# Experts in a fixed order with 8 KB weight pieces and pads, and eight modulation blocks moved from beside attention

## The chip, the cores and the metric

The kernel runs on one core of one Trainium2 chip. The metric is the time of one execution on the device in microseconds (us). Times of several runs are given by their median, with the lowest and the highest. Profiles are of one execution each. The engines are PE (TensorE; PEld is its weight load), DVE (VectorE), ACT (ScalarE), POOL (GpSimd) and SP (SyncE, which here only issues transfers).

## The reference

Two blocks of a network in float32 on 512 tokens of width 1024. The first: modulated norm, differential attention of 4 heads over 768 keys, a Fourier mix, and 32 experts with two chosen per token. The second: an S5 mixer with a gated linear unit (glu), an MLP, an SSD mixer and a second MLP, each behind a modulated norm. Cut to what the change touches:

```python
def expert_block(args):
    tok, wt, e = args
    xb = h_pad[tok]
    y = (jax.nn.silu(xb @ w_gate[e]) * (xb @ w_up[e])) @ w_down[e]
    return y * wt[:, None]
...
out = jnp.zeros((t + 1, d), ys.dtype).at[buf_tok].add(ys.reshape(-1, d))
...
mod = cond @ ada_w[i] + ada_b[i]
sh1, sc1, g1, sh2, sc2, g2 = jnp.split(mod[:, None, :], N_MOD, axis=-1)
h = _modulate(_rmsnorm(x, norm_mix_g[i]), sh1, sc1)
...
ab = g @ w_glu.astype(f32) + b_glu.astype(f32)
val, gate = jnp.split(ab, 2, axis=-1)
return (val * jax.nn.sigmoid(gate)).astype(h.dtype)
```

`w_gate` and `w_up` are 32 x 1024 x 512, `w_down` is 32 x 512 x 1024, `ada_w` is 2 x 1024 x 6144.

## The kernel before, in words

The program runs its stages one after the other: `pre` (modulation, the input projection, attention, Fourier mix, output projection, router), `moe` (the experts), `end_first` (the first block's result is transposed and normed), `s5` with the glu, an MLP, the SSD mixer, an MLP, and the last norm.

**The experts** (`moe`, L916). They are taken in 16 pairs; two pairs make a step `st` of four experts. Each expert has 64 places for tokens, so a pair fills 128: expert A the columns 0 to 63 of PE's array, B the columns 64 to 127, with a matmul of its own for each (L970, L1001: "tiled"). A pair's work on PE, with the names that the profile shows: `G` and `U` (the products with gate and up, 32 records each: an fp32 matmul is two), `phT` (L982, four transposes of the gated product), `pw` (L988, each place's gate weight), `Y` (L1001, the products with down in two halves of 512 columns), `pohT` (L1012, four transposes of the one-hot matrix), and the combine `pcmb` (L1019, L1020): eight output blocks of two matmuls, each added by DVE to the residual `x` (L1022). ACT copies between them: `sg` (L978), `hT` (L984), `yh` (L1006), `ohT` (L1014). The second pair of a step also gathers the tokens of the next step, `pg` (L910, L911): four quarters of 16 matmuls, which ACT copies to `xg` with scale and shift (L914).

**What lies beside the experts.** A generator `self.blocks` (`s5_blocks`, L1496) makes tables for the S5 stage, one block per pair. It has three small groups on PE, `pcd`, `pm` and `pkt` (L1518, L1543, L1550), table work on DVE (`m`, `pb`, `tmpm`), copies `Cd`, `me` and `kt` on ACT, and stores by POOL's queue.

**What sets the order.** The code states data dependencies and the framework's scheduler places each engine's instructions, so groups of one pair and of the next are mixed. `issue_after` holds an item back behind a named instruction. PSUM has eight banks: in this stage one pool of 7 for all products and one bank, `psz`, for `pcd`, `pm`, `pkt` and the modulation.

**Weights.** `raw` (L125) takes a slot of a ring of six (8 KB per partition each) and issues the load on SP (L127). A 1 MB load of an expert's half matrix takes rows as `(k p)`: 512 runs of 2 KB, four to each partition. The first two loads of `w_down` go to two buffers `extra` (L937).

**Modulation** (`ada_quads`, L350). The first block's modulation and that of the second block's first layer are products of a vector with a 1024 x 6144 matrix, in blocks of 512 columns: four loads of 512 KB (tile `adaw`, 1 KB runs) and for each four matmuls `ada` (L364; 8 records). The generator `self.side` yields once per block; `values`, `keys`, `queries` and `attention` take one at each `next`, so that these loads and matmuls lie beside attention. Their buffers, `adap`, are two. `glu` (L1739) follows products of `gemm_T` (L162) on `w_s_glu`, 48 matmuls each.

## Time and profile before

| | us |
|---|---|
| median of 3 runs (lowest to highest) | 2454.11 (2452.0 to 2458.82) |
| the profiled execution | 2456.05 |
| its span | 2454.3 |
| PE busy | 2281.1 (93%) |
| DVE busy | 1353.9 (55%) |
| ACT busy | 816.7 (33%) |
| POOL busy | 240.2 (10%) |
| moved by DMA | 454.02 MB, 185 GB/s over the span |

Times in the trace count from the start of the span. A record's busy time includes what overlaps its neighbours (matmuls are pipelined), so the pace of matmuls is read from start to start. The chain that ended last lies for 54% of the span on PE. The page's shares are means over stages with different limits, so each stage is read by itself. "Idle before, and the releaser" in a row says what an engine was waiting for: a wait for several things is put down to the one that came last. SP's waits are for free buffers.

### The profile page before, as it was taken

Reading aid. Unit: us, or ns where it says so; the run is one execution under the profiler, and the core shown is the slowest. Engines: PE = TensorE matmul, PEld = TensorE weight load, DVE = VectorE, ACT = ScalarE, POOL = GpSimd, SP = SyncE. Lnnn points to the kernel's source line nnn. Section 1 sums busy time; section 2 is a strip of 40 time slices with the busy share of each in tenths; the row PEclk is TensorE's granted clock in tenths of the full one; section 3 lists DMA queues with packets and bytes.
Section 4 is the critical chain, followed back from the end, with each engine's and each line's share of the span. In section 5 each row is a group of like instructions: output and inputs, shape, how many; then the busy total and the mean of one; then the engine's idle time right before and its main releaser. Section 6 shows DMA issues by size and latency. Waiting matters only on the chain.

```text
span 2454.3 us, 32253 instructions
## 1 busy us (share of the span) xinstructions
PE 2281.1 (93%) x12503; PEld 1633.9 (67%) x12503; DVE 1353.9 (55%) x2583; ACT 816.7 (33%) x1317; POOL 240.2 (10%) x407
## 2 busy tenths in 40 slices
PE   7988999699998999979999999999999998999997
PEld 4664569344444444368788778787778777888787
DVE  4754445424334242466667884466786778544454
ACT  4232343211111111154333332335654434322332
POOL 0166000011111010000000000000221210000000
PEclk9899999899999999989999999999999999999999
DMA  8577645699999999945545772342332322233330
GB/s 282 163 219 235 196 141 189 248 326 341 355 377 322 331 331 355 340 132 160 175 125 169 228 229 91 95 123 62 112 104 87 111 78 86 69 95 95 94 96 35
DMA packets 327775, 454.02 MB, mean 185 GB/s; under 512 B 22308, under 2 KB 201252, under 8 KB 327620
## 3 DMA queue, kind: packets, MB, share of 16 engines
q1 hardware_dynamic: 318272, 435.23, 53.8%
q0 software_dynamic: 8592, 16.27, 2.1%
q8 instruction: 100, 1.64, 0.3%
q10 hardware_dynamic: 756, 0.43, 0.1%
q14 instruction: 55, 0.45, 0.1%
HBM read 436.14 MB, written 15.73 MB: 184 GB/s over the span
## 4 chain that ended last, share of the span: by engine, by line
PE 54%; DVE 8%; DMA 3%; ACT 3%; issue 2%; POOL 0%; SPq 0%; DVEq 0%; ACTq 0%; POOLq 0%
PE pt L146 13%; PE pt L147 13%; PE pt L148 13%; PE G L970 3%; PE Y L1001 3%; PE U L970 3%; DMA adaw<-in_ada_w 3%; DVE adaacc L314 1%; DVE wl L140 1%; PE pg L910 1%; PE pg L911 1%; PE py L1925 1%; PE pY L1668 0%; DVE x L1327 0%; PE pG L1637 0%
## 5 line engine op out<-in xcount | busy, mean ns | idle before, releaser
L140 DVE TENSOR_TENSOR wl<-w,wh 128x1024 fp32r<-128x1024 f32 (+2 forms) x239 | 287.4, 1207 | 225.1 <-ACT wh L139 221.0
L139 ACT ACTIVATE wh<-w 128x1024 fp32r<-128x1024 f32 (+1 forms) x241 | 249.0, 1040 | 480.5 <-PE pt L147 375.1
L146 PE MATMUL pt<-hh,wh 128*128 128x512 f32 (+2 forms) x976 | 369.0, 383 | 3.2 <-ACT hh L1219 3.0
L147 PE MATMUL pt<-hl,wh 128*128 128x512 f32 (+2 forms) x976 | 367.9, 380 | 0.1
L148 PE MATMUL pt<-hh,wl 128*128 128x512 f32 (+2 forms) x976 | 365.9, 378 | 0.0
L146 PE MATMUL pt<-ab,wh 128*128 128x512 f32 (+1 forms) x576 | 213.4, 375 | 4.8 <-ACT o L1347 2.9
L147 PE MATMUL pt<-ab,wh 128*128 128x512 f32 (+1 forms) x576 | 214.4, 373 | 1.1 <-DVE ab L1296 0.9
L148 PE MATMUL pt<-ab,wl 128*128 128x512 f32 (+1 forms) x576 | 213.7, 372 | 0.0
L146 PEld LDWEIGHTS pt<-hh,wh 128*128 128x128 f32 (+1 forms) x976 | 181.9, 188 | 44.9 <-ACT hh L1219 4.2
L147 PEld LDWEIGHTS pt<-hl,wh 128*128 128x128 f32 (+1 forms) x976 | 182.9, 188 | 39.3 <-issue 3.6
L148 PEld LDWEIGHTS pt<-hh,wl 128*128 128x128 f32 (+1 forms) x976 | 183.0, 188 | 39.0 <-issue 3.5
L1327 DVE SCALAR_TENSOR_TENSOR x<-pt,mod,x 128x512 f32<-128x512 f32 (+1 forms) x184 | 122.3, 678 | 115.2 <-PE pt L148 114.5
L970 PE MATMUL G<-w,xg 128*64 128x512 f32 x512 | 131.8, 602 | 5.3 <-DVE x L1022 5.3
L979 DVE TENSOR_TENSOR sg<-sg,U 128x512 f32<-128x512 f32 x16 | 11.0, 688 | 227.6 <-PE U L970 227.6
L970 PE MATMUL U<-w,xg 128*64 128x512 f32 x512 | 131.1, 594 | 0.0
L146 PEld LDWEIGHTS pt<-ab,wh 128*128 128x128 f32 x576 | 108.2, 190 | 30.2 <-ACT ab L1295 7.6
L147 PEld LDWEIGHTS pt<-ab,wh 128*128 128x128 f32 x576 | 109.4, 190 | 23.3 <-DVE ab L1296 3.5
L148 PEld LDWEIGHTS pt<-ab,wl 128*128 128x128 f32 x576 | 109.3, 190 | 19.9
L1914 POOL TENSOR_TENSOR ec<-ec,BC 128x384 f32<-128x384 f32 x32 | 39.9, 1263 | 686.7 <-PE pt L148 571.3
L970 PEld LDWEIGHTS G<-w,xg 128*64 128x64 f32 x512 | 38.0, 137 | 75.9 <-issue 63.0
L970 PEld LDWEIGHTS U<-w,xg 128*64 128x64 f32 x512 | 40.8, 137 | 70.7 <-issue 69.2
L1022 DVE TENSOR_TENSOR x<-x,pcmb 128x512 f32<-128x512 f32 x128 | 80.5, 673 | 4.7 <-PE pcmb L1020 4.7
(575 smaller groups left out, 4236.5 us busy)
## 6 DMA issues: line engine op xcount, KB each, us to landing
w<-in_w_gate SPq DMA_DIRECT2D x64, 1024.0 KB
w<-in_mlp_w SPq DMA_DIRECT2D x128, 512.0 KB
w<-in_w_up SPq DMA_DIRECT2D x63, 1024.0 KB
extra<-in_w_down SPq DMA_DIRECT2D x32, 1024.0 KB
w<-in_w_down SPq DMA_DIRECT2D x31, 1024.0 KB
adaw<-in_ada_w SPq DMA_DIRECT2D x48, 512.0 KB
adaw<-in_ada_w SPq DMA_DIRECT2D x96, 256.0 KB
w<-in_m_w_in SPq DMA_DIRECT2D x40, 512.0 KB
```

The lines of the kernel that those rows point to most:

```text
L139: nc.scalar.activation(h, w, AF.Copy)
L140: (eng or nc.vector).tensor_tensor(l, w, h.bitcast(F32), op=SUB)
L146: nc.tensor.matmul(out, ah, bh, start=start, stop=False, skip_group_check=True)
L147: nc.tensor.matmul(out, ah, bl, start=False, stop=False, skip_group_check=True)
L148: return nc.tensor.matmul(out, al, bh, start=False, stop=stop, skip_group_check=True)
L314: nc.vector.scalar_tensor_tensor(acc, w, ck, acc, op0=MUL, op1=ADD)
L910: nc.tensor.matmul(pt[:, i], self.h2h[:, t, ks], oh2d[:, t], start=(t == 0), stop=False)
L970: nc.tensor.matmul(pt[64 * i:64 * i + 64], xg[:, kh * 4 + k, so + 64 * i:so + 64 * i + 64], ws[i][:, k], start=(kh == 0 and k == 0), stop= ...
L1001: ip = nc.tensor.matmul(pt[64 * i:64 * i + 64], hT[:, k, 64 * i:64 * i + 64], ws[i][:, k], start=(k == 0), stop=(k == 3), tile_position=(0 ...
L1022: nc.vector.tensor_tensor(xs, xs, pt, op=ADD)
L1327: self.nc.vector.scalar_tensor_tensor(xs, src, gate, xs, op0=MUL, op1=ADD)
L1914: nc.gpsimd.tensor_tensor(ec, ec, BC[:, 1, 128:512], op=MUL)
```

## The change

Four parts.

1. **8 KB pieces.** Row `d` of a matrix is now `p*8+k` (`p*4+k` for down), so that a partition's part of a half matrix is one run of 8 KB, 128 runs for a megabyte. A half of `w_down` is now half of its rows at full width, so both Y banks fill together and end together. The order of rows inside the operands follows: `h2h`, `h2l` are written from strided reads, the scale and shift columns are turned through a transpose and a DRAM tile, `hm` reads `sg` and `U` with stride 4.
2. **Fixed order.** Each PE instruction of the experts and the S5 blocks gets, by `pin`, a dependency without a semaphore on the one before it in the program. The combine of a pair moves into the next pair: two output blocks after each of the four half products of G and U. `pw` moves behind the first half of G, in fp32r with the weights split in two (four matmuls in one pass in place of four in two). Two gather quarters lie in each pair, one before and one after `phT` (none in the first pair, four in the second, none in the last two). `pohT` is a product with an fp32r identity. S5 blocks are yielded in thirds. PSUM: tag `a` 2 banks, `gu` 3 (G, U, Y), `c` 2 (combine), `psz` 1.
3. **Modulation.** Of the 12 blocks of the second block's first layer eight leave attention: four loads behind the transposes in `end_first`, four before the first S5 scan, and eight after each of three glu products. They take slots of the weights' ring (`rawp`). What stays is taken four loads at a time, at half of attention's places.
4. **Pads.** Small tiles `shift`, `shift2`, `shift3` move the addresses of what follows them.

```diff
+    def pin(self, i):
+
+        if self.pinned:
+            if self.line is not True:
+                self.tc.add_manual_dep(i.ins, self.line.ins.name, mybir.DependencyInfo(
+                    mybir.DependencyClass.NoSync, mybir.DependencyReason.DATA), reason="pin")
+            self.line = i
+        return i
...
-    def ada_quads(self, items):
+    def ada_quads(self, items, tile, total):
...
-                        w = self.adap.tile([128, 4, 256], F32, tag="w", name="adaw")
+                        w = tile()
...
+                        if (b, k0, hf) != (nb - 1, 4, 1):
+                            yield
...
+    def sides(self, n):
+        for _ in range(n):
+            next(self.side, None)
...
-        ada = [(a["w_ada"][0], 0, n, mcol[:, n * 4 - 16:n * 4], self.col["bada"][:, n * 4:n * 4 + 16]) for n in (4, 8)]
-        ada += [(a["ada_w_2"][0], 1, n, mod0[:, n * 4:n * 4 + 16], self.col["bada0"][:, n * 4:n * 4 + 16]) for n in (0, 4, 8)]
+        ada = [(a["w_ada"][0], 0, n, 4, mcol[:, n * 4 - 16:n * 4], self.col["bada"][:, n * 4:n * 4 + 16]) for n in (4, 8)]
+        ada0 = [(a["ada_w_2"][0], 1, n, m, mod0[:, n * 4:(n + m) * 4], self.col["bada0"][:, n * 4:(n + m) * 4])
+                for n, m in ((0, 4), (4, 2), (6, 4), (10, 2))]
...
-        next(self.blocks)
+        for _ in range(4):
+            next(self.blocks)
...
+        pt = self.psum_z((16, 128), name="psp")
+        nc.tensor.transpose(pt, mcol[:, 8:24], self.ident)
+        rows = tp.tile([16, 128], F32, tag="ssr", name="ssr", bufs=1)
+        nc.scalar.activation(rows, pt, AF.Copy)
+        ssd = self.dr.tile([16, 128], F32, name="ssd")
+        nc.sync.dma_start(ssd, rows)
+        ssp = self.g.tile([128, 2, 8], F32, name="ssp")
+        nc.sync.dma_start(ssp, ssd.rearrange("(c r) (q k) -> (r q) c k", c=2, k=8))
+        self.sh2, self.sc2 = ssp[:, 0], ssp[:, 1]
...
+        xk = lambda t, k: x1[:, t].rearrange("s (p k) -> s k p", k=8)[:, k]
+        by_k = lambda h, t, k: h[:, t].rearrange("s (k p) -> s k p", k=8)[:, k]
...
+        self.mods2_scale(0, mod0, 8, "nmix")
+
+        self.side = self.ada_quads(ada0[1:], lambda: self.rawp.tile([128, 4, 256], F32, tag="raw", name="adaw"),
+                                   lambda: self.nrm.tile([128, 512], F32, tag="sq", name="adaacc"))
...
-                next(self.side, None)
+                self.sides(4)
...
-            next(self.side, None)
+            if t % 2 == 0:
+                self.sides(4)
...
         def part(wt, e, kh, q=None):
-            return self.raw(wt[e, kh * 512:(kh + 1) * 512].rearrange("(k p) n -> p k n", p=128), (128, 4, 512), q=q)
+            return self.raw(wt[e].rearrange("(p k) n -> p k n", k=8)[:, 4 * kh:4 * kh + 4], (128, 4, 512), q=q)
...
-        down = lambda e, hf: wd[e, :, hf * 512:(hf + 1) * 512].rearrange("(k p) n -> p k n", p=128)
+        down = lambda e, kh: wd[e].rearrange("(p k) n -> p k n", k=4)[:, 2 * kh:2 * kh + 2]
         xg2 = self.B((128, 2, 2048), name="xg")
-        place = lambda w: w.rearrange("p (k n) -> p k n", k=4)
+        place = lambda w: w.rearrange("p (k n) -> p k n", k=2)
...
-                return self.raw(down(e, hf), (128, 4, 512))
+                return self.raw(down(e, hf), (128, 2, 1024))
...
+            gu = lambda n: self.ps.tile([128, 512], F32, tag="gu", name=n, bufs=3)
+            pin = self.pin
+            self.line = self.pinned = True
...
+            def combine(ohT, yh, yl):
+
+                for t in range(4):
+                    for hf in range(2):
+                        pt = self.ps.tile([128, 512], F32, tag="c", name="pcmb")
+                        ls = ohT[:, t * 128:(t + 1) * 128]
+                        pin(nc.tensor.matmul(pt, ls, yh[:, hf], start=True, stop=False))
+                        pin(nc.tensor.matmul(pt, ls, yl[:, hf], start=False, stop=True))
+                        xs = x1[:, t, hf * 512:(hf + 1) * 512]
+                        nc.vector.tensor_tensor(xs, xs, pt, op=ADD)
+                        yield
...
+            ident_r = mp.tile([128, 128], F32R, name="ident_r", bufs=1)
+            nc.scalar.activation(ident_r, self.ident, AF.Copy)
+
+            gw2 = mp.tile([128, 4, 8, 2, 4], F32R, name="gw2", bufs=1)
+            gw4 = self.gw.rearrange("p t (s e) -> p t s e", e=4)
+            nc.scalar.activation(gw2[:, :, :, 0], gw4, AF.Copy)
+            nc.vector.tensor_tensor(gw2[:, :, :, 1], gw4, gw2[:, :, :, 0].bitcast(F32), op=SUB)
...
+                    quarters = [(nxt[1], nxt[0], 256, (k, k + 2)) for k in range(0, 8, 2)] if st < 7 else []
+                    quarters = quarters[2 * pr:2 * pr + 2] if st else quarters[:4 * pr]
+                    G, U = gu("G"), gu("U")
...
-                                    nc.tensor.matmul(pt[64 * i:64 * i + 64], xg[:, kh * 4 + k, so + 64 * i:so + 64 * i + 64],
-                                                     ws[i][:, k], start=(kh == 0 and k == 0), stop=(kh == 1 and k == 3),
-                                                     tile_position=(0, 64 * i), skip_group_check=True)
-                    for i in range(4):
-                        if pr == 1 and st < 7:
-                            self.gather(nxt[1], nxt[0], 256, (2 * i, 2 * i + 2))
-                    sg = mp.tile([128, 512], F32, tag="sg", name="sg")
-                    hm = sg
+                                    pin(nc.tensor.matmul(pt[64 * i:64 * i + 64],
+                                                         xg[:, kh * 4 + k, so + 64 * i:so + 64 * i + 64], ws[i][:, k],
+                                                         start=(kh == 0 and k == 0), stop=(kh == 1 and k == 3),
+                                                         tile_position=(0, 64 * i), skip_group_check=True))
+                            for _ in range(2):
+                                next(back, None)
+                            if (w is wg) and kh == 0:
+
+                                pw = self.psum((128, 2, 4), name="pw")
+                                for t in range(4):
+                                    pin(nc.tensor.matmul(pw, oh2[:, t, so:so + 128], gw2[:, t, st], start=(t == 0), stop=(t == 3)))
+                                wv = mp.tile([128, 1], F32, tag="wv", name="wv", bufs=4)
+                                for i in range(2):
+                                    ps = slice(64 * i, 64 * i + 64)
+                                    nc.vector.tensor_reduce(wv[ps], pw[ps, :, 2 * pr + i], axis=AX.X, op=ADD)
+                    sg = mp.tile([128, 512], F32, tag="sg", name="sg", bufs=1)
+                    hm = mp.tile([128, 4, 128], F32, tag="y", name="hm")
+                    k4 = lambda ap: ap.rearrange("s (p k) -> s k p", k=4)
                     nc.scalar.activation(sg, G, AF.Silu)
-                    nc.vector.tensor_tensor(hm, sg, U, op=MUL)
+                    nc.vector.tensor_tensor(hm, k4(sg), k4(U), op=MUL)
+
+                    pt = self.psum(name="pohT")
...
+                        pin(nc.tensor.matmul(pt[:, t * 128:(t + 1) * 128], oh2[:, t, so:so + 128], ident_r, start=True,
+                                             stop=True, skip_group_check=True))
+                    ohT = mp.tile([128, 512], F32R, tag="ohT", name="ohT", bufs=1)
...
+                    half = len(quarters) // 2
+                    for q in quarters[:half]:
+                        self.gather(*q)
...
-                        nc.tensor.transpose(pt[:, k * 128:(k + 1) * 128], hm[:, k * 128:(k + 1) * 128], self.ident)
-                    hT = mp.tile([128, 4, 128], F32, tag="hT", name="hT", bufs=1)
+                        pin(nc.tensor.transpose(pt[:, k * 128:(k + 1) * 128], hm[:, k], self.ident))
...
-                    pw = self.psum((128, 4), name="pw")
-                    for t in range(4):
-                        nc.tensor.matmul(pw, oh2[:, t, so:so + 128].bitcast(F32), self.gw[:, t, e0:e0 + 4],
...
+                    for q in quarters[half:]:
+                        self.gather(*q)
+                    if eA:
+                        for _ in range(2):
+                            next(self.blocks, None)
...
+                    Y = [gu("Y") for _ in range(2)]
+                    for kh in range(2):
+                        ws = [ahead.pop((id(wd), kh, i)) if eA == 0 and (id(wd), kh, i) in ahead else
+                              part_d(eA + i, kh, None if kh else own[i]) for i in range(2)]
+                        for hf in range(2):
+                            for k in range(2):
+                                for i in range(2):
+                                    pin(nc.tensor.matmul(Y[hf][64 * i:64 * i + 64], hT[:, 2 * kh + k, 64 * i:64 * i + 64],
+                                                         ws[i][:, k, hf * 512:(hf + 1) * 512], start=(kh == 0 and k == 0),
+                                                         stop=(kh == 1 and k == 1), tile_position=(0, 64 * i),
+                                                         skip_group_check=True))
...
-                    with tc.issue_after(ia.ins), tc.issue_after(iv.ins), tc.issue_after(ip.ins):
+                    with tc.issue_after(ia.ins), tc.issue_after(iv.ins):
...
+                    back = combine(ohT, yh, yl)
+            for _ in back:
+                pass
+            self.line = self.pinned = None
...
+        with self.tc.issue_after(it.ins):
+            self.sides(4)
...
+            yield
...
+            yield
...
+        self.sides(4)
...
-        for n in range(1, 3):
-            pv, pg = [self.gemm_T(wglu, 0, c0 + n * 256, [(gx, 512)])[0] for c0 in (0, D)]
-            glu(n, slice(0, 512), pv, pg)
+
+        cols = [c0 + n * 256 for n in (1, 2) for c0 in (0, D)]
+        units = list(self.wunits(wglu, 0, cols[0]))
+        for i, c in enumerate(cols):
+            cur, units = units, list(self.wunits(wglu, 0, cols[i + 1])) if i < 3 else None
+            ps = (ps if i % 2 else []) + self.gemm_T(wglu, 0, c, [(gx, 512)], units=cur)
+            if i % 2:
+                glu(1 + i // 2, slice(0, 512), *ps)
+            if i < 3:
+                self.sides(8)
+        for _ in self.side:
+            pass
+        self.mods2_scale(0, mod, 32, "nmlp")
...
+            self.tp.tile([128, 56], F32, name="shift2", bufs=1)
...
-            self.ps = self.pool(c2, "psm", 7, space=PSUM)
+            self.ps = self.pool(c2, "psm", 2, space=PSUM)
```

PE's order in the instruction streams, at the seam between two pairs of experts, before (`pm` and `pkt` are S5's; `pb` and `m` its tables):

```order
L1543 MATMUL pm_4524<-cst,pb 128x128 x4
L1019 MATMUL pcmb<-yh,ohT 128x512
L1020 MATMUL pcmb<-yl,ohT 128x512
L970 MATMUL G<-w,xg 64x512
L1550 MATMUL pkt<-m_4516,pb 16x128 x4
L1551 MATMUL pkt<-dd,cst 16x4x16
L970 MATMUL G<-w,xg 64x512 x15
L970 MATMUL U<-w,xg 64x512 x16
```

There the combine ends ahead of G, and `pkt` stands inside G. PE's order at the same seam now:

```order
L1602 MATMUL pcd<-cst,cr 64x64 x2
L1032 MATMUL G<-w,xg 64x512 x8
L996 MATMUL pcmb<-yh,ohT 128x512
L997 MATMUL pcmb<-yl,ohT 128x512
L996 MATMUL pcmb<-yh,ohT 128x512
L997 MATMUL pcmb<-yl,ohT 128x512
L1042 MATMUL pw<-gw_4144,oh 128x8 x4
L1032 MATMUL G<-w,xg 64x512 x8
L996 MATMUL pcmb<-yh,ohT 128x512
L997 MATMUL pcmb<-yl,ohT 128x512
L996 MATMUL pcmb<-yh,ohT 128x512
L997 MATMUL pcmb<-yl,ohT 128x512
L1032 MATMUL U<-w,xg 64x512 x8
```

G now starts first, and the combine, of the pair before, has moved between the halves of G and U; `pm` and `pkt` have moved behind the gather.

SP's order at the glu's weights before (`m` and `cs` are S5 tables, `in_mlp_w_2` is the next stage's weights):

```order
L1611 DMA m_9130<-s5d_0_812 128x1024
L1614 DMA cs<-s5c_814 64x2x512 x2
L1618 DMA m_9129<-s5k_790 16x8x128 x8
L1620 DMA m_9131<-s5d_1_813 128x1024
L127 DMA w<-in_s_w_glu 128x4x256 x12
L127 DMA w<-in_mlp_w_2 128x4x256 x12
L309 DMA adaw<-in_ada_w 128x512 x6
```

The twelve loads of the glu stand together. SP's order at the same place now (`adaw` is a modulation load):

```order
L1707 DMA m_9008<-s5d_1_815 128x1024
L129 DMA w<-in_s_w_glu 128x4x256 x4
L373 DMA adaw<-in_ada_w 128x4x256 x8
L129 DMA w<-in_s_w_glu 128x4x256 x2
L373 DMA adaw<-in_ada_w 128x4x256 x8
L129 DMA w<-in_s_w_glu 128x4x256 x2
L373 DMA adaw<-in_ada_w 128x4x256 x8
L129 DMA w<-in_s_w_glu 128x4x256 x4
L129 DMA w<-in_mlp_w_2 128x4x256 x12
```

Eight modulation loads now stand between the loads of two products, on the queue that feeds both.

PE's order where the first block ends, from the last combine to the first S5 products `pk`, before:

```order
L1020 MATMUL pcmb<-yl,ohT 128x512
L1139 MATMUL xp<-cst,x_3304 128x128 x32
L1183 MATMUL bc<-cst,rqy 128x128 x8
L146 MATMUL pk<-wh,hh 128x256
L147 MATMUL pk<-wl,hh 128x256
```

The transposes `xp` and the norm's broadcast `bc` follow each other. PE's order at the same place now:

```order
L997 MATMUL pcmb<-yl,ohT 128x512
L1219 MATMUL xp<-cst,x_3106 128x128 x32
L375 MATMUL ada<-adaw,scp 32x256 x16
L1266 MATMUL bc<-cst,rqy 128x128 x8
L157 MATMUL pk<-wh,hh 128x256
L158 MATMUL pk<-wl,hh 128x256
```

The matmuls of four modulation loads (16) have moved in between `xp` and `bc`.

## Rows read from the trace of the kernel before

**Rows 1.** Timeline of PE, start and end of the experts: start us, us, instruction [idle before <-releaser].
```profile
451.27 1.94 PE L970 MATMUL G<-w,xg 128*64 128x512 f32 x8
...
1060.62 0.39 PE L1019 MATMUL pcmb<-yh,ohT 128*128 128x512 f32 x1
1060.85 0.40 PE L1020 MATMUL pcmb<-yl,ohT 128*128 128x512 f32 x1
```

**Rows 2.** Lines of PE, 500 to 1000: busy us, mean ns | idle before <-releasers.
```profile
L970 PE MATMUL G<-w,xg 128*64 128x512 f32 x408 | 105.4, 602 | 4.8 <-DVE x L1022 4.8
...
L1019 PE MATMUL pcmb<-yh,ohT 128*128 128x512 f32 x104 | 41.5, 424 | 12.7 <-ACT ohT L1014 8.9 <-ACT yh L1006 3.8
...
L1543 PE MATMUL pm<-cst,pb 128*128 128x128 f32 x52 | 8.2, 280 | 13.0 <-DVE pb L1538 13.0
L982 PE MATMUL phT<-cst,sg 128*128 128x128 f32 x52 | 8.1, 279 | 5.5 <-DVE sg L979 5.5
```

**Rows 3.** Waits of SP's queue, 500 to 1000: us in total, times, longest us.
```profile
SPq L127 <- PE G L970: 167.1, 50, 12.5
```

**Rows 4.** Windows: us, then busy of PE, PEld, DVE, ACT, POOL, PEclk, DMA share, GB/s.
```profile
500.00:1000.00 500.00, 461.44 (x2300) 222.29 (x2298) 179.57 (x344) 86.50 (x172) 72.75 (x123) 0.99 0.96 341
```

**Rows 5.** The same view, an undisturbed stretch of the experts.
```profile
645.00:667.00 22.00, 21.63 (x134) 13.13 (x132) 1.03 (x4) 5.16 (x10) 0.00 (x0) 1.00 1.05 388
```

**Rows 6.** Timeline of PE, starts of three pairs following each other.
```profile
637.68 1.07 PE L970 MATMUL G<-w,xg 128*64 128x512 f32 x2 [0.53 <-DVE x L1022]
...
678.24 1.07 PE L970 MATMUL G<-w,xg 128*64 128x512 f32 x2 [0.53 <-DVE x L1022]
...
712.76 1.07 PE L970 MATMUL G<-w,xg 128*64 128x512 f32 x2 [0.53 <-DVE x L1022]
713.76 1.05 PE L1550 MATMUL pkt<-m,pb 128*16 128x128 f32 x8
...
714.95 1.51 PE L970 MATMUL G<-w,xg 128*64 128x512 f32 x6
```

**Rows 7.** Timeline of PE, gather and Y in a pair that gathers.
```profile
653.75 0.39 PE L910 MATMUL pg<-oh,h2h 128*128 128x256 f32 x1
...
661.51 0.60 PE L982 MATMUL phT<-cst,sg 128*128 128x128 f32 x4
661.95 0.95 PE L988 MATMUL pw<-gw,oh 128*128 128x4 f32 x8
...
666.75 3.60 PE L1001 MATMUL Y<-w,hT 128*64 128x512 f32 x16
670.29 0.30 PE L1518 MATMUL pcd<-cst,cr 64*64 64x64 f32 x2
```

**Rows 8.** Timeline of PE, U in a pair whose gather lies in pieces.
```profile
802.28 3.65 PE L970 MATMUL U<-w,xg 128*64 128x512 f32 x14
...
806.53 1.07 PE L970 MATMUL U<-w,xg 128*64 128x512 f32 x2
...
810.00 3.65 PE L970 MATMUL U<-w,xg 128*64 128x512 f32 x14
```

**Rows 9.** Lines of ACT, 500 to 1000.
```profile
L914 ACT ACTIVATE xg<-pg,mcol 128x256 f32<-128x256 f32 x56 | 28.5, 559 | 84.7 <-PE pg L911 84.7
```

**Rows 10.** DMA queues, 717 to 718: packets, MB, share of 16 engines.
```profile
q0 software_dynamic: 63, 0.26, 64.1%
q1 hardware_dynamic: 81, 0.16, 42.0%
```

**Rows 11.** Lines of PE, 230 to 345.
```profile
L364 PE MATMUL ada<-adaw,scp 128*32 128x256 f32 x304 | 26.1, 391 | 10.2 <-DMA adaw<-in_ada_w 9.8
```

**Rows 12.** Windows, the same stretch.
```profile
230.00:345.00 115.00, 105.20 (x717) 64.15 (x717) 44.03 (x106) 40.46 (x90) 6.01 (x8) 1.00 0.66 207
```

**Rows 13.** Timeline of PE, between the experts and S5.
```profile
1069.21 2.82 PE L1139 MATMUL xp<-cst,x 128*128 128x128 f32 x12 [4.15 <-ACT x L1144]
1072.61 1.77 PE L1183 MATMUL bc<-cst,rqy 128*128 128x128 f32 x8 [0.58 <-DVE rqy L212]
```

**Rows 14.** Windows, the glu's products.
```profile
1201.00:1256.00 55.00, 54.86 (x249) 44.32 (x250) 30.89 (x34) 24.61 (x29) 0.00 (x0) 1.00 0.45 138
```

More of the change, by code (lines that the diff above doesn't have):

```diff
@@ L496, in pre @@
         s5p = self.pool(c3, "s5p", 1, side="right")
-        self.side = self.ada_quads(ada)
+        self.side = self.ada_quads(ada + ada0[:1], lambda: self.adap.tile([128, 4, 256], F32, tag="w", name="adaw"),
+                                   lambda: tp.tile([128, 512], F32, tag="ada", name="adaacc"))
         self.att_setup(at)
@@ L909, in gather @@
                 for t in range(4):
-                    nc.tensor.matmul(pt[:, i], self.h2h[:, t, ks], oh2d[:, t], start=(t == 0), stop=False)
-                    nc.tensor.matmul(pt[:, i], self.h2l[:, t, ks], oh2d[:, t], start=False, stop=(t == 3))
+                    self.pin(nc.tensor.matmul(pt[:, i], self.h2h[:, t, ks], oh2d[:, t], start=(t == 0), stop=False))
+                    self.pin(nc.tensor.matmul(pt[:, i], self.h2l[:, t, ks], oh2d[:, t], start=False, stop=(t == 3)))
             for i in range(per):
@@ L1023, in moe @@
+            for _ in back:
+                pass
+            self.line = self.pinned = None
         self.tap("x2pre", x1)
@@ L1694, in s5 @@
         pr = {0: prepare(0)}
+        self.sides(4)
         st = {0: scan(0, *pr[0])[0]}
```

120 lines of the change are left out of this document (52 added, 68 removed).

## The prediction

> **What bounds the kernel now.** I began with the experts, the longest stage: its first G product starts at 451.3 us and its last combine ends at 1061.2 [rows 1], 610 us of the 2454.3 us span. The reader is to see in that stage who waits for whom. PE has idle time before four kinds of work, each time for DVE or ACT [rows 2]; no row names a transfer. SyncE in turn stands for PE: 167 us of the 500 us from 500 to 1000 for G alone [rows 3], because it can't issue a weight load until a product has freed its slot. So PE's order of work sets the end and the DMA engines follow, but not by much: they move 341 GB/s on average there [rows 4], and 388 GB/s where nothing disturbs them [rows 5]. A faster PE therefore finds at most 388/341, some 12% of the stage, before the transfers hold it.
>
> **A pair of experts, in PE's rows.** Two pairs in sequence start at 637.68, 678.24 and 712.76 [rows 6]: 40.6 us for one that also gathers the next four experts' tokens, 34.5 us for one that doesn't. I rebuild it from starts in the rows. Sixteen records of Y take 670.29 - 666.75 = 3.54 us [rows 7], so G, U and Y, of 32 records each, take 21.2. A combine matmul takes 0.23 [rows 1], sixteen 3.7. pw takes 0.95 [rows 7], pkt 1.19 (713.76 to 714.95) [rows 6], the 14 small matmuls and transposes of pm, phT, pohT and pcd, at the gather's interval of 0.12, 1.7. A change between whole-array work and the products on half the columns shows in 712.76 to 713.76: two records of G in 1.00 us instead of 0.44, so 0.56 more [rows 6]; three more changes in a pair make 1.7. That is 30.4 us. The four waits sum to 36.0 us in 500 us [rows 2], at 38.1 us a pair (610/16) 2.75 each: 33.2, against 34.5 measured. A gather of 64 matmuls runs from 653.75 to 661.51, 7.76 us [rows 7]; 33.2 + 7.8 is 41.0, against 40.6. Seven of 16 pairs gather, so the rebuilt stage is 16 x 33.2 + 7 x 7.8 = 586 us, 24 short of the 610. Part of the 24 is seen in a gather laid in pieces between products: U is broken at 806.53 and again at 810.00 [rows 8], each break two more changes.
>
> **Fixed order.** What goes: all four waits. The combine stands behind half a product (3.5 us), longer than ACT's copy of yh or ohT; phT stands behind pohT and a gather quarter; pm behind the second; G behind nothing that DVE still owes. That takes off 16 x 2.75 = 44 us. pw has four records in place of eight, 0.48 a pair: 8 us. What comes: one more change of mode a pair, since the combine now cuts G and U into halves (into a tiled product five times a pair, four before): 16 x 0.56 = 9 us. Two new waits: the general PSUM tag has two banks, so the second gather quarter waits until ACT has copied the first, two copies of 0.56 [rows 9] less the 0.5 of phT between them, with the hand-over about 0.9; and pkt has the single psz bank that pm used, behind ACT's two xg copies and me (about as long as an xg), less pm itself, about 1.3. Fourteen pairs have gather quarters: 14 x 2.2 = 31 us. The nearest rows bound a new wait from below by zero, where the copies are done in time, and from above by 1.0 to 1.3 for each of five turns, the size of the waits that now show. The number of gather quarters is the same, 28. Rebuilt: 44 + 8 - 9 - 31 = 12 us less. Of the 24 us that the rebuilding misses I take 17 off, because no quarter cuts a product any more, and keep 7 as mishaps that recur. **Experts: 29 us less**, from 610 to 581, or 36.3 a pair.
>
> The Trainium skill speaks against the interleaving (TensorEngine Tiling (Array Packing), section Key Properties): a change of tiling mode drains TensorE. The rows agree that a change costs, 0.56 us here; by that rule alone, five changes for four, this part would be 9 us slower.
>
> **8 KB pieces.** The byte count is the same, 12.6 MB a pair. The trace has no 8 KB packets. The nearest: in one microsecond 63 packets of 4 KB filled 64.1% of 16 engines' time, 0.163 us each, 402 GB/s by all 16, and 81 packets of 2 KB filled 42.0%, 0.083 us, 395 GB/s [rows 10]. So doubling the run gave 2%, and I take 8 KB as 0 to 5% better. With 12.6 MB of weights and some 0.8 MB of S5 blocks, 36.3 us a pair asks 369 GB/s, inside 388. Credit of its own: none, since PE is the later; but it is what lets the gain above be had. The reordering of rows for it (strided reads in h2h, h2l, hm, a 16 x 128 transpose and a trip of the scale and shift through DRAM) lies ahead of the experts beside the router or on engines that wait: 0 to 3 us, I take 0. The pads move addresses only: 0, and nothing bounds them but the sum.
>
> **Modulation.** Between 230 and 345 us, 304 records of `ada` are 38 loads (8 records each), busy 26.1 us, 0.69 a load, and PE waits 9.8 us for their weights [rows 11]; PE is busy 105.2 of the 115 us [rows 12], so these waits are all the idle time there is, and the stage is PE's. Taking 32 loads away saves 32 x 0.69 = 22 us and 32/38 of the waits, 8: 30 us. If ACT's softmax shows up in their place it is less, at worst 15. They return at three places. Four behind the transposes xp: PE idles there for 4.15 us at one wait [rows 13], but bc and the first S5 products stand behind them and 2 MB precede S5's own loads on SyncE: 3 us. Four before the first scan: 2.8. Twenty-four between the glu's products, which leave PE no gap (54.9 of 55 us busy, 138 GB/s) [rows 14]: 24 x 0.69 = 16.6, and waits: the stage's 7.6 MB become 20.2 in some 72 us, 280 GB/s, through six ring slots and in 1 KB pieces. At the waits of attention, 0.26 a load, 6 us; from below 0, from above 25, where the engines bring no more than the 207 GB/s of attention's stretch [rows 12]. Sum: -30 + 3 + 2.8 + 16.6 + 6, **2 us less**.
>
> **Sum.** 2456.05 - 29 - 2 = 2425 for the profiled execution, which is 2 us above the median of the runs, so **2423** against 2454.11.
>
> **Rivals.**
> *The new waits don't show.* ACT is busy for 86.5 of 500 us in the stage [rows 4], and the copies may come early. Then 31 us more go: 2392. Against it: the second quarter's bank is read by two copies that can't begin before the first quarter ends.
> *Transfers hold.* If 8 KB pieces, 16 KB apart in DRAM, come no faster than today's mean of 341 GB/s [rows 4], a pair needs 13.4 MB / 341 = 39 us and the experts stay where they are; with the modulation's 2 us, 2452. For it: the DMA engines are already busy at a share of 0.96 on average [rows 4]. Against it: 388 GB/s at 1.05 for 22 us on end [rows 5], and SyncE that waits for slots, so loads come before they are wanted. The Trainium skill (DMA: Bandwidth & Descriptors, Specifications) puts HBM at about 358 GB/s for a core; by that, an estimate, a pair would take 37.4 us and the time be some 2441. The trace shows more than 358 on 2 KB pieces, so the measurement decides.
> *Slower: the pinned order turns every PSUM turn into idle PE.* The free order before let PE do something else (Y around pohT, G around pkt); a pinned one can't. pohT, two quarters, phT, pm and pkt share two banks and one. It decides at 2.2 us of new waits a pair beyond the 2.2 that I count, where the gain of 31 is gone; at five turns of 1.3 us and one of 0.6, 7.1 a pair, the experts lose 14 x 4.9 = 69 us on my sum: 2492.
> *The glu starves.* Its waits at the upper end, 19 us more than I take: 2442, inside the range.
>
> **How the numbers follow.** The measurement can tell 0.3%, 7 us, from no change: faster is below 2446.7, slower above 2461.5. Forecast, 2407 to 2440 with its bounds: 0.47. New waits hidden: 0.24. Transfers hold: 0.16, of it 0.05 faster, 0.09 the same and 0.02 slower. Pinned order slower: 0.13, of it 0.02 the same and 0.11 slower. So faster 0.76, same 0.11, slower 0.13. The range takes in the second case with some of the attention's waits (2375) and the third (2458), and leaves the slower one out.
>
> **What would show it.** In the new profile: a pair of 36 us without the 40/34 alternation; no idle time before pcmb, phT and G; in its place idle before pg with ACT xg and before pkt with ACT me named; five tiled starts a pair; the DMA line near 370 GB/s. Between 150 and 345 a stage shorter by 25 to 30 us, and a glu longer by 17 to 25 with `adaw` named as releaser. The prediction is wrong if PE's waits in the experts name `w` by DMA, if pairs stay at 38, or if attention gives back less than 15.

## The result, and the profile after

The changed kernel takes 2384.41 us (median of 4 runs, 2382.98 to 2387.81) against 2453.06 us before on the same chip: a ratio of 0.9724, 95% interval 0.9695 to 0.9753. That is 69 us less; 31 were forecast. The time lies in the range that was given and on the side that was forecast, but the gain is more than twice the forecast, so several terms of the sum were wrong. The profiled execution has a span of 2383.3 us, 71.0 less than the one before.

Where the 71 us are, stage by stage. The ends of the stages are read from PE's timeline in both traces: first router product `plg`, first G, last `pcmb`, first `pk` of S5, last `pgT`, last product of the glu, the last product of the first MLP, of the SSD mixer, PE's last instruction (9 us of the span follow it in both).

| stage | before, us | after, us | difference | forecast |
|---|---|---|---|---|
| start to router | 408.9 | 381.8 | -27.1 | -30 |
| router to first G | 42.3 | 50.4 | +8.1 | 0 |
| experts | 610.0 | 554.6 | -55.4 | -29 |
| end of first block | 15.3 | 12.1 | -3.2 | +3 |
| S5 scans | 123.5 | 135.1 | +11.6 | +2.8 |
| glu | 76.6 | 93.3 | +16.7 | +22.6 |
| first MLP | 380.7 | 374.2 | -6.5 | 0 |
| SSD mixer | 410.5 | 403.5 | -7.0 | 0 |
| second MLP and end | 377.4 | 369.4 | -8.0 | 0 |

The last three lines, 21.5 us, lie in stages in which the change edits nothing but a pad.

One pair of experts in the timeline of PE after (start, duration, instruction [idle before <-releaser]):

```profile
709.09 3.65 PE L1032 MATMUL G<-w,xg 128*64 128x512 f32 x16
712.67 0.50 PE L996 MATMUL pcmb<-yh,ohT 128*128 128x512 f32 x1
...
713.70 0.50 PE L1042 MATMUL pw<-gw,oh 128*128 128x8 f32 x4
714.13 3.65 PE L1032 MATMUL G<-w,xg 128*64 128x512 f32 x16
717.71 0.50 PE L996 MATMUL pcmb<-yh,ohT 128*128 128x512 f32 x1
...
718.84 3.65 PE L1032 MATMUL U<-w,xg 128*64 128x512 f32 x16
722.43 0.50 PE L996 MATMUL pcmb<-yh,ohT 128*128 128x512 f32 x1
...
723.55 3.65 PE L1032 MATMUL U<-w,xg 128*64 128x512 f32 x16
```

Half a product takes 3.58 us every time (712.67 - 709.09), and the four groups of the combine between them 1.03 to 1.13. Nothing waits. The pairs that gather two quarters follow each other at 34.9 us, where [rows 6] had 40.6 and 34.5 in turn.

The lines of PE over the experts, 432.2 to 986.9 (busy us, mean ns | idle before <-releasers), those with idle time and products (two lines with 0.7 us idle each are left out):

```profile
L1032 PE MATMUL G<-w,xg 128*64 128x512 f32 x512 | 116.9, 599 | 0.0
L1032 PE MATMUL U<-w,xg 128*64 128x512 f32 x512 | 116.7, 598 | 0.0
L943 PE MATMUL pg<-oh,h2h 128*128 128x256 f32 x241 | 61.0, 291 | 8.8 <-ACT xg L947 8.8
...
L996 PE MATMUL pcmb<-yh,ohT 128*128 128x512 f32 x128 | 57.7, 451 | 1.6 <-ACT yh L1088 0.8 <-DVE x L999 0.7
L1081 PE MATMUL Y<-w,hT 128*64 128x512 f32 x248 | 57.6, 592 | 0.0
...
L1635 PE MATMUL pkt<-m,pb 128*16 128x128 f32 x120 | 15.7, 274 | 16.6 <-ACT me L1629 16.6
L1064 PE MATMUL phT<-cst,hm 128*128 128x128 f32 x64 | 9.7, 274 | 0.7 <-DVE hm L1051 0.7
```

The same view of the kernel before, 451.3 to 1061.2, for the two products:

```profile
L970 PE MATMUL G<-w,xg 128*64 128x512 f32 x512 | 131.8, 602 | 5.3 <-DVE x L1022 5.3
L970 PE MATMUL U<-w,xg 128*64 128x512 f32 x512 | 131.1, 594 | 0.0
```

The four waits of [rows 2] are gone but for 2 to 3 us; the two that were forecast have come, 8.8 and 16.6. But 29 us went where nobody waited: the same 512 records of G are busy 116.9 us in place of 131.8, those of U 116.7 in place of 131.1.

And a stretch of the first MLP, PE's timeline, before:

```profile
1529.82 0.40 PE L146 MATMUL pt<-hh,wh 128*128 128x512 f32 x1
1530.05 0.40 PE L147 MATMUL pt<-hl,wh 128*128 128x512 f32 x1
...
1531.22 0.40 PE L146 MATMUL pt<-hh,wh 128*128 128x512 f32 x1
```

and after:

```profile
1474.77 0.39 PE L157 MATMUL pt<-hh,wh 128*128 128x512 f32 x1
1474.99 0.39 PE L158 MATMUL pt<-hl,wh 128*128 128x512 f32 x1
...
1476.13 0.39 PE L157 MATMUL pt<-hh,wh 128*128 128x512 f32 x1
```

Six products take 1.40 us before and 1.36 after: 233 ns and 227 ns from start to start. The code, the shapes and the granted clock are the same.

### The profile page after: what moved, and what is told of

It is laid out like the page before. It is cut to its first block, busy times and chain, and to the rows that moved or that the text cites. A ratio compares the mean times of both kernels' runs of the same rounds, so it can differ in the third digit from the quotient of the medians.

```text
span 2383.3 us, 32069 instructions
## 1 busy us (share of the span) xinstructions
PE 2222.9 (93%) x12448; PEld 1624.1 (68%) x12448; DVE 1363.7 (57%) x2585; ACT 819.1 (34%) x1321; POOL 237.1 (10%) x407
## 4 chain that ended last, share of the span: by engine, by line
PE 64%; DVE 7%; ACT 4%; DMA 3%; issue 2%; POOL 0%; SPq 0%; DVEq 0%; ACTq 0%; POOLq 0%
PE pt L157 13%; PE pt L158 12%; PE pt L159 12%; PE U L1032 5%; PE Y L1081 5%; PE G L1032 4%; DMA adaw<-in_ada_w 3%; PE pcmb L996 2%; PE pg L943 2%; PE pg L944 1%; PE pcmb L997 1%; DVE adaacc L325 1%; ACT wh L141 1%; DVE wl L142 1%; DVE q L1376 1%
## 5 line engine op out<-in xcount | busy, mean ns | idle before, releaser
L157 PE MATMUL pt<-hh,wh 128*128 128x512 f32 (+2 forms) x976 | 363.8, 378 | 3.2 <-ACT hh L1302 3.0
L158 PE MATMUL pt<-hl,wh 128*128 128x512 f32 (+2 forms) x976 | 362.5, 374 | 0.0
L159 PE MATMUL pt<-hh,wl 128*128 128x512 f32 (+2 forms) x976 | 360.6, 372 | 0.1
L1032 PE MATMUL G<-w,xg 128*64 128x512 f32 x512 | 116.9, 599 | 0.0
L1032 PE MATMUL U<-w,xg 128*64 128x512 f32 x512 | 116.7, 598 | 0.0
L943 PE MATMUL pg<-oh,h2h 128*128 128x256 f32 x256 | 66.8, 297 | 21.2 <-DVE oh L930 12.4
L1032 PEld LDWEIGHTS U<-w,xg 128*64 128x64 f32 x512 | 34.1, 136 | 66.9 <-issue 62.2
```

What stands on the lines that cost most here:

```text
L157: nc.tensor.matmul(out, ah, bh, start=start, stop=False, skip_group_check=True)
L158: nc.tensor.matmul(out, ah, bl, start=False, stop=False, skip_group_check=True)
L159: return nc.tensor.matmul(out, al, bh, start=False, stop=stop, skip_group_check=True)
L943: self.pin(nc.tensor.matmul(pt[:, i], self.h2h[:, t, ks], oh2d[:, t], start=(t == 0), stop=False))
L1032: pin(nc.tensor.matmul(pt[64 * i:64 * i + 64], xg[:, kh * 4 + k, so + 64 * i:so + 64 * i + 64], ws[i][:, k], start=(kh == 0 and k == 0), s ...
```

## The experiments

All times are medians, with the ratio to the kernel before on the same chip, which is the better number to compare (the kernel before itself had medians from 2450 to 2459 us). A stage that no edit touches also moves by some us from profile to profile: the first MLP takes 374.2 us in the change and up to 378.8 in kernels with the same pads.

**Without the pads.**

```diff
-        self.g.tile([128, 8], F32, name="shift")
-            self.tp.tile([128, 56], F32, name="shift2", bufs=1)
-        pool.tile([128, 40], F32, name="shift3", bufs=1)
```

> The change without its three pads. Theory A (pads set the pace of the wide products: in the MLPs the median start-to-start time of a 512-column product is 233 to 234 ns before and 226 to 227 ns after the change, and no other part of the change touches that stage): the pace returns to 233 or more, the two MLPs and the SSD mixer take back the 22 us that they lost, total 2405 to 2412 us. Rival B (the pace comes from the new layout of pools around the experts, the pads are for nothing): 2384 us within 7, the pace stays at 226.

2403.03 us, ratio 0.9787 (0.976 to 0.9815). The pace is 234 ns again; the MLPs take 380.4 and 377.1 us, the SSD mixer 407.3, the experts 554.3 as with pads. 17.7 us come back in these three stages, so theory A, though the total lies 2 us below its range. The pads are a term of the sum and not a free edit.

**Small pieces.** Gate and up in 2 KB, down in 4 KB runs, rows in their old order:

```diff
-            return self.raw(wt[e].rearrange("(p k) n -> p k n", k=8)[:, 4 * kh:4 * kh + 4], (128, 4, 512), q=q)
+            return self.raw(wt[e, kh * 512:(kh + 1) * 512].rearrange("(k p) n -> p k n", p=128), (128, 4, 512), q=q)
...
-        self.sh2, self.sc2 = ssp[:, 0], ssp[:, 1]
+        self.sh2, self.sc2 = sh2, sc2
```

> The change with pieces of 2 KB for gate and up and 4 KB for down, and no reordered rows. The stage asks some 13.4 MB in 34.9 us, 384 GB/s. Theory A (8 KB pieces are what lets PE's order pay): with 2 KB pieces the trace before never moved more than 388 GB/s undisturbed and 341 on average, so PE waits for weights, pairs go to 36 to 38 us, the experts lose 20 to 45 us and the router gains back 7.5: 2397 to 2422 us. Rival B (transfers follow PE anyway): pairs stay at 34.9 us, and the strided reads that the order of rows needs ahead of the experts are saved, 2377 us.

2380.82 us, ratio 0.9703 (0.9678 to 0.9728). The experts take 553.1 us with pairs of 34.9, so rival B: at this pace the small pieces keep up. Router to first G takes 42.5 us, as before the change, in place of 50.4: the order of rows that 8 KB pieces need costs 8 us there. (The total doesn't show these 8 us: the intervals of the two ratios overlap.) The windows of 480 to 930, small pieces and then the change:

```profile
480.00:930.00 450.00, 427.19 (x2212) 204.00 (x2210) 179.97 (x343) 82.39 (x165) 72.67 (x123) 1.00 1.02 376
```

```profile
480.00:930.00 450.00, 426.05 (x2232) 207.59 (x2232) 183.15 (x342) 86.31 (x173) 73.19 (x124) 1.00 0.95 374
```

The same GB/s at a DMA share of 1.02 against 0.95: the larger pieces have room left, which nothing asks for yet.

**Without the pin.**

```diff
-            self.line = self.pinned = True
+            self.line = self.pinned = None
```

> The change without the chain of dependencies that pins PE's order; everything else as it is. Theory A (the pinned order is what removed the waits): the scheduler mixes pairs again, pairs go back to 37 us or more, experts lose 25 to 50 us, 2410 to 2435 us. Rival B (the program's own new order and the PSUM tags do it, the chain is idle): 2384 us within 7.

2462.41 us, ratio 1.003 (1.0014 to 1.0046): the whole gain and more is lost. The experts take 630.0 us, with pairs of 41.2. It is more than either theory gave, and it isn't waiting: PE's idle time in the experts is 31 us, 29 in the change. The lines of PE over the experts of this run:

```profile
L1032 PE MATMUL G<-w,xg 128*64 128x512 f32 x512 | 142.4, 601 | 0.0
L1032 PE MATMUL U<-w,xg 128*64 128x512 f32 x512 | 129.1, 597 | 0.0
L1081 PE MATMUL Y<-w,hT 128*64 128x512 f32 x248 | 77.5, 601 | 0.0
```

G, U and Y are again busy for longer with the same records (this line of Y: 57.6 us in the change). The timeline shows why:

```profile
817.52 1.07 PE L1032 MATMUL G<-w,xg 128*64 128x512 f32 x2
818.53 0.50 PE L997 MATMUL pcmb<-yl,ohT 128*128 128x512 f32 x1
...
820.47 3.65 PE L1032 MATMUL G<-w,xg 128*64 128x512 f32 x14
824.05 0.50 PE L996 MATMUL pcmb<-yh,ohT 128*128 128x512 f32 x1
```

The scheduler has put a combine between expert A's matmul (two records) and expert B's. The two records alone take 1.01 us, and the other fourteen 3.58, as long as sixteen undivided. A and B, on two halves of the array, run beside each other only when they stand next to each other. A run of records is what lies between two pieces of other work; whole A-B pairs make runs that divide by four. Of the runs of G, U and Y, 56 of 68 don't hold whole pairs before (2 and 62 records, for instance), 76 of 125 here, and none of 78 in the change.

**Modulation back beside attention.**

```diff
-                for n, m in ((0, 4), (4, 2), (6, 4), (10, 2))]
+                for n, m in ((0, 4), (4, 4), (8, 4))]
...
-        self.side = self.ada_quads(ada + ada0[:1], lambda: self.adap.tile([128, 4, 256], F32, tag="w", name="adaw"),
+        self.side = self.ada_quads(ada + ada0, lambda: self.adap.tile([128, 4, 256], F32, tag="w", name="adaw"),
```

> The change with the eight modulation blocks back beside attention. Between start and router the change saved 27 us, the first S5 scans lost 11.6 us, the glu 16.7. Theory A (moving them is near to neutral, as the sum of these terms says): 2384 us within 8. Rival B (most of the gain of 27 us came from elsewhere, so the move is a loss): the attention grows by less than 15 us and the time falls to 2360 to 2375 us. Rival C (attention takes the whole 27 back and S5 and the glu give less): 2395 us or more.

2393.54 us, ratio 0.9755 (0.973 to 0.9779). Start to router 413.0 us (31.2 more than in the change), S5 120.9 (14.2 less), glu 76.9 (16.4 less). The three terms cancel to under 1 us in the profiles, as theory A says. The median lies between the bounds of A (2392) and of rival C (2395): by the ratios moving the blocks gains 8 us, and their intervals overlap, so a small gain is neither shown nor excluded. Rival B fell.

**What a change of mode costs, and what a torn pair.** pw's four matmuls moved into the first half of G, behind an even or an odd number of tiled matmuls (the even case; `i == 0` in the odd):

```diff
+                                    if w is wg and kh == 0 and k == 1 and i == 1:
+                                        pw = self.psum((128, 2, 4), name="pw")
...
-                            if (w is wg) and kh == 0:
-
-                                pw = self.psum((128, 2, 4), name="pw")
```

> The change with pw's four matmuls moved from behind the first half of G into it, behind the fourth of its eight matmuls, so between two complete pairs (A, B) of tiled matmuls: one more change between tiled and whole-array work in each pair of experts, nothing else. Theory A (a change costs little, 0.2 to 0.3 us; what cost 0.56 in the rows of before was a matmul of expert A alone, without B beside it): 16 pairs x 0.25, 4 us more than the change, pairs of 35.1 to 35.2 us. Theory B (the prediction's price, 0.56 us for each change): 9 us more, pairs of 35.5 us.

> The same, but pw lies one matmul earlier, between the matmul of expert A and that of B: as many changes of mode as in the even case, and one pair of tiled matmuls torn apart. Theory A: a tiled matmul alone takes as long as the two side by side, 0.43 us lost, so pairs are 0.4 to 0.5 us longer than in the even case and the time 6 to 8 us above it. Theory B: the same time as the even case.

Even: 2402.3 us, ratio 0.9802 (0.9773 to 0.983); odd: 2406.11 us, ratio 0.9815 (0.9788 to 0.9842). The totals hold more than the edit, since other stages took longer in these runs as well (the first MLP 378.7 and 376.8 us); the pairs tell it apart. They are 35.4 us in the even case and 36.2 in the odd one, 34.9 in the change; the experts take 565.5, 574.5 and 554.6. PE's timeline, even:

```profile
709.86 1.94 PE L1032 MATMUL G<-w,xg 128*64 128x512 f32 x8
711.73 0.61 PE L1039 MATMUL pw<-gw,oh 128*128 128x8 f32 x4
712.27 1.94 PE L1032 MATMUL G<-w,xg 128*64 128x512 f32 x8
714.13 0.50 PE L996 MATMUL pcmb<-yh,ohT 128*128 128x512 f32 x1
```

and odd:

```profile
719.96 1.93 PE L1032 MATMUL G<-w,xg 128*64 128x512 f32 x6
721.82 0.61 PE L1039 MATMUL pw<-gw,oh 128*128 128x8 f32 x4
722.36 2.79 PE L1032 MATMUL G<-w,xg 128*64 128x512 f32 x10
725.08 0.50 PE L996 MATMUL pcmb<-yh,ohT 128*128 128x512 f32 x1
```

Six records take 1.86 us, as long as eight, and ten take 2.72: the torn pair costs 0.85 us (5.12 against 4.27 from the first G to the combine), twice what theory A gave it. The even excursion, which is a change to whole-array work and back, costs 0.35 in these rows (1.87 + 1.86 for 3.58, pw and combine 0.1 longer each) and 0.5 in the pair. So A is right that a torn pair is a cost of its own and B falls in the odd case; in the even case the price of a change was nearer to B's 0.56 than to A's. The four combine groups of the change are cheaper: 14.32 us for G and U and about 4.4 for the combine, against an estimated 14.16 and 3.7 without any excursion (4 x 3.54 from [rows 7], 16 x 0.23 from [rows 1]), so 0.2 each.

**The wait of pkt taken away.** pm goes ahead of the second gather quarter, so that ACT has copied me before pkt wants the bank:

```diff
-        for _ in range(4):
+        for _ in range(5):
             next(self.blocks)
...
+                    if eA:
+                        next(self.blocks, None)
                     for q in quarters[half:]:
                         self.gather(*q)
...
             nc.scalar.activation(me, pt, AF.Copy)
+            yield
```

> The change with S5's transposes pm moved ahead of the second gather quarter, so that ACT's copy me is done when pkt wants the bank: takes away the wait of pkt for me, 16.6 us in 15 waits, the largest one left among the experts. Theory A (PE's order is still the bound): pairs of 33.8 us, 13 to 16 us less than the change, 2369 us. Rival B (the transfers are now the bound: 13.4 MB in 33.8 us ask 396 GB/s): the wait comes back as PE waiting for w, pairs stay at 34.5 to 34.9, 2380 us or more.

2364.41 us, ratio 0.9634 (0.9602 to 0.9666): the fastest kernel of the study, 20 us below the change (22 by the ratios). Pairs are 33.3 us, the experts 533.5; the wait of pkt is 1.5 us in all, and that of pg fell too, 8.8 to 3.1, since pm now lies in it. Theory A: PE's order was still the bound. The window of 480 to 930 now moves 395 GB/s at a share of 1.00:

```profile
480.00:930.00 450.00, 446.17 (x2338) 217.63 (x2336) 190.06 (x350) 89.34 (x179) 74.29 (x126) 1.00 1.00 395
```

**The same with small pieces.**

> The same with pieces of 2 KB for gate and up and 4 KB for down and no reordered rows. Theory A (8 KB pieces matter only once PE's pair is shorter than 34.5 us, what 388 GB/s allow): pairs of 34.5 us here against 33.8 with 8 KB pieces, with PE waiting for w; the experts 8 to 12 us longer than with 8 KB pieces, of which the router gives 7.5 back. Rival B (small pieces keep up at any pace): pairs of 33.8 us and 5 to 8 us less in all than with 8 KB pieces.

2369.01 us, ratio 0.9658 (0.9629 to 0.9686). Pairs begin at 33.3 us and lie between 33.5 and 35.7 from the sixth on (the last of all takes 31.0); the experts take 547.0, 13.5 more than with 8 KB pieces, and router to first G 44.0, 6.5 less. The totals of the two runs don't tell them apart (their intervals overlap); the experts do. U's line over the experts with 8 KB pieces, then U's lines on PE and PEld with small ones (432 to 985), a late product in the timeline (669 to 676), and the window:

```profile
L1032 PE MATMUL U<-w,xg 128*64 128x512 f32 x512 | 116.7, 598 | 0.0
```

```profile
L1032 PE MATMUL U<-w,xg 128*64 128x512 f32 x512 | 128.7, 599 | 1.0 <-DMA w<-in_w_up 0.8
```

```profile
L1032 PEld LDWEIGHTS U<-w,xg 128*64 128x64 f32 x512 | 38.3, 136 | 75.7 <-issue 57.9 <-DMA w<-in_w_up 10.4 <-PE pcmb L997 5.4
```

```profile
669.87 4.68 PE L1032 MATMUL U<-w,xg 128*64 128x512 f32 x16
670.89 0.20 PEld L1032 LDWEIGHTS U<-w,xg 128*64 128x64 f32 x4 [0.84 <-DMA w<-in_w_up]
```

```profile
480.00:930.00 450.00, 445.63 (x2255) 211.15 (x2254) 182.97 (x348) 85.08 (x172) 73.70 (x125) 1.00 1.03 382
```

U is busy 12 us longer than with 8 KB pieces. PE's own line shows little of it as idle, because A's matmul runs alone, and counts as busy, until B's weights land; the weight loads of U wait 10.4 us for the transfer. Theory A: 8 KB pieces matter from the pace at which small ones, at 382 GB/s and a share of 1.03, have nothing left.

**Which starts set the pace of the wide products.** Five kernels: the kernel before with one pad of 32 bytes a partition, the change with both operands or the stationary one alone moved by 32 bytes, and the kernel before with pads of 96 and 224 bytes.

```diff
         self.g = self.pool(ctx, "glob", 1)
+        self.g.tile([128, 8], F32, name="shift")
```

```diff
-        self.g.tile([128, 8], F32, name="shift")
...
+        self.pool(self.ctx, "rpad", 1, side="right").tile([128, 8], F32, name="rshift")
         self.wp = self.pool(self.ctx, "wp", 2, side="right")
```

> The kernel before with one pad of 32 bytes a partition and nothing else. It moves the moving operands of nearly all 512-column products from a start that is a multiple of 64 bytes to 32 past one; the stationary operands stay at 32 past one. Theory A (these starts set the pace): 233 to 234 ns a product become 226 to 227 in the MLPs, the time 15 to 22 us less than before, 2432 to 2439 us, and the experts stay at 610 us. Rival B (the pads help only together with the new layout): no difference, 2454 us within 7.

> The change with moving and stationary operands both starting at multiples of 64 bytes. Theory A (the pace depends on whether the two starts are alike modulo 64): 226 to 227 ns a product. Theory B (the moving operand must start at 32 past a multiple of 64): 233 to 234 ns.

> The change with the moving operands left at 32 past a multiple of 64 bytes and the stationary ones moved to a multiple of 64. Theory A (starts must be alike): 233 to 234 ns a product. Theory B (only the moving operand counts): 226 to 227 ns.

> The kernel before with one pad of 96 bytes a partition in place of 32, and nothing else. With 32 bytes, moving and stationary operands were alike modulo 64 and the pace stayed at 233 ns, so likeness modulo 64 isn't enough. With 96 bytes they start alike modulo 256 in nine of ten 512-column products. Theory A (alike modulo 128 or 256 is what counts, in any kernel): 226 to 227 ns a product in the MLPs, 15 to 22 us less than before, 2432 to 2442 us. Rival B (something else of the new layout sets the pace): 233 ns, no difference.

> The same with a pad of 224 bytes: the operands start alike modulo 128 and 128 apart modulo 256. Theory A1 (modulo 128 counts): 226 to 227 ns a product. Theory A2 (modulo 256 counts): 233 to 234 ns.

The starts are those of the built program, in bytes within the partition; the pace is the median start to start of the `pt` products with 512 columns in the whole trace, counted where another `pt` product follows at once.

| kernel | moving operand mod 256 | stationary operand mod 256 | products of that kind | ns |
|---|---|---|---|---|
| before | 128 | 224 | 3830 | 234 |
| before, few products | 224 | 224 | 275 | 227 |
| change | 224 | 224 | 4206 | 227 |
| without pads | 192 | 224 | 3931 | 234 |
| both moved | 192 | 192 | 4206 | 227 |
| stationary moved | 224 | 192 | 4090 | 234 |
| before, 32-byte pad | 160 | 224 | 3830 | 233 |
| before, 96-byte pad | 224 | 224 | 3830 | 227 |
| before, 224-byte pad | 96 | 224 | 3830 | 232 |

Times: 32-byte pad 2455.71 us, ratio 0.9986 (0.9966 to 1.0006), no change, as its rival B had it. Theory A fell in that form, because starts alike modulo 64 aren't enough, and the next pads decide against rival B. Both moved 2383.68 and stationary moved 2401.98, one run each; 96-byte pad 2437.54, ratio 0.9923 (0.989 to 0.9957), 19 us less with nothing but a pad; 224-byte pad 2458.81, one run. Theory A2 holds in all nine lines: 227 ns where the two operands start alike modulo 256 bytes, 232 to 234 where they don't. The 275 products of the second line follow it as well: where a pad, or taking the pads away, makes their starts unlike (0, 32, 64 or 192 against 224), they take 229 to 235. The rest of the trace agrees: first MLP, SSD mixer and second MLP together take 1147 to 1154 us in the profiles of all ten kernels with starts alike, 1165 to 1171 in the five others. One group stands apart: 144 products of the first block lie mostly between 224 and 240 ns in the change, though alike. PE's timeline of the kernel before with the 96-byte pad:

```profile
1529.83 0.39 PE L147 MATMUL pt<-hh,wh 128*128 128x512 f32 x1
...
1531.19 0.39 PE L147 MATMUL pt<-hh,wh 128*128 128x512 f32 x1
```

## Why the prediction was wrong, by its steps

**What bounds the experts: right.** PE's order was the bound and the transfers follow: without the pin 75 us are back, and the two waits that the early pm cuts, by 15.1 and 5.7 us, shorten the stage by 21.1. The rival in which transfers hold at 341 GB/s fell, with 374 in the window of the change. The ceiling given by 388 GB/s was near: the small pieces met theirs at 382 one step later, and 8 KB pieces moved 395.

**The waits: right.** 44 us of waits were to go and 31 to come. Idle time in the experts was 48.2 us (5.3 + 17.6 + 14.6 + 8.1 + 2.6 in the lines of the whole stage); 25.4 came at the two places that were named, and 3.7 are left at the others. The rival in which these two don't show (2392) came near in time and is wrong in cause: they do show. That the measured time lies near it is luck. The pinned order's further waits, the slower rival, didn't come.

**The price of a change of mode, the step that failed in the experts.** The prediction read 712.76 to 713.76 in [rows 6] as two records that should take 0.44, so 0.56 for a change of mode, and booked a fifth one a pair as a loss. Those two records are expert A's matmul torn from B's: alone they take 0.86 us (2.72 - 1.86 in the odd split), and 0.14 is left for the change. In the changed kernel an excursion of the combine costs 0.2. The work of a pair with two quarters is 33.1 us (34.9 less 1.8 of waits) where 34.4 were booked: 16 x 1.3, 21 us of the 26 that the forecast of the stage lacked. The rebuilt old pair was also added up wrong: four changes were named and its 30.4 us hold three; with the fourth it is 31.0, and the stage 15 us short of the 610 instead of 24. That rest was put down to cut products and mishaps. Torn pairs explain it better, by an estimate that no run splits further: the old order has 56 torn runs, so 28 torn pairs, and at 0.85 us each 24 us in all, part of it booked as changes of mode. The rows of before already showed that two records of G alone take 1.00 us and not 0.44.

The Trainium skill's rule (TensorEngine Tiling (Array Packing), section Key Properties), that a change of tiling mode drains TensorE, agrees with the 0.2 to 0.5 us per excursion. The same section says that different tiles can execute matmuls in parallel; the odd split agrees and shows what that is worth here, 0.85 us when it is broken once.

**The pads: wrong, from 0 to about 18 to 20 us.** "0, and nothing bounds them but the sum" was no bound. The trace of before held the evidence: 275 of its 512-column products ran at 227 ns beside 3830 at 234. Nobody asked why equal instructions have two paces.

**The order of rows: wrong, from 0 to 8 us.** It was said to lie beside the router. The lines of ACT and DVE show `h2h` at 2123 ns in place of 1136 and `h2l` at 1123 in place of 740 (two lines of before, then two of after); with small pieces and the old order of rows they are at 1133 and 743 again. The router's own small steps queue behind `h2h` on ACT, and the gather behind `h2l`:

```profile
L615 ACT ACTIVATE h2h<-x,rqy 128x1024 fp32r<-128x1024 f32 x4 | 4.4, 1136 | 2.6 <-DVE rqy L212 2.6
```

```profile
L620 DVE SCALAR_TENSOR_TENSOR h2l<-x,rqy,h2h 128x512 fp32r<-128x512 f32 x8 | 5.5, 740 | 0.0
```

```profile
L645 ACT ACTIVATE h2h<-x,rqy 128x1024 fp32r<-128x1024 f32 x4 | 8.3, 2123 | 2.6 <-DVE rqy L223 2.6
```

```profile
L650 DVE SCALAR_TENSOR_TENSOR h2l<-x,rqy,h2h 128x512 fp32r<-128x512 f32 x8 | 8.5, 1123 | 0.0
```

The window of that stage has PE busy for 25.8 of 50.4 us, where it was 24.5 of 42.4, and its granted clock at 0.66 where it was 0.72: of its two levels, 1.2 and 2.4 GHz, PE had the lower one for longer.

**The modulation: the sum right, its terms not all.** -27.1 - 3.2 + 11.6 + 16.7 is 2 us less, as forecast, but that the misses cancel is luck. The glu's waits were 0.9 us, not 6:

```profile
L375 PE MATMUL ada<-adaw,scp 128*32 128x256 f32 x192 | 13.1, 386 | 0.9 <-DMA adaw<-in_ada_w 0.9
```

Behind `xp` the added matmuls cost nothing, and the stage's granted clock rose from 0.78 to 1.00. The S5 scans took 11.6 us more in place of 2.8: PE's idle time there is 18.8 us in place of 13.2 and its granted clock 0.90 in place of 0.93. The loss goes away with the blocks (120.9 us when they are back), but whether the loads on SyncE or the matmuls cause it wasn't tried.

**8 KB pieces: right that they earn nothing by themselves;** wrong that the experts' gain hung on them. It does only at the next step, at pairs of 33.3 us, where they are worth 13.5 us of the experts.

## What to carry to other kernels

Two tiled products that share the array earn their speed only as neighbours: count the runs of records between other work, and where a scheduler may put something between the two, pin them. Price an interruption from a row in which the pair is whole. Before a pad or a layout is booked at nothing, look whether equal instructions have one pace in the trace; two paces are a question about addresses. And a new layout in memory is paid by whoever writes it, ahead of the stage that reads it.

## What was not expected of the hardware

A 512-column fp32r product takes 227 ns from start to start where its moving and stationary operands start alike modulo 256 bytes of the partition, and 229 to 235 ns otherwise, mostly 232 to 234: 3%, seen in the nine lines above, and 19 us of this kernel by a pad of 96 bytes. Products with 256 columns don't follow it (120 ns in the change, 119 before). Why isn't known from these runs.
